# Hybrid RG-LRU and pooling layer: bias sums formed from the other side and at other places, opening matmuls reordered, last output blocks finished another way

## The chip, the core and the metric

The kernel runs on one core of one Trainium2 chip. The metric is device time in microseconds (us) of one execution of the whole kernel, as the median of several runs.

## What is computed

One layer with 1024 frames, a model width of 1024 and float32 data. The reference, cut to its core:

```python
h = x @ w_in + b_in                       # 1024 x 6144: xa | za | xb | zb | ga | gb
xa = causal_conv4(xa)
ya = RG_LRU(xa) * silu(za)                # gates, then a scan along the frames
yb = multiscale_pool(xb) * silu(zb)       # windows 2, 4, 8, 16
merged = sigmoid(ga) * (ya @ w_proj_a) + sigmoid(gb) * (yb @ w_proj_b)
y = merged @ w_out + b_out
out = layer_norm(alpha * x + y)           # alpha = 2 ** 0.25, gain and bias rows
```

So there are nine products of 1024x1024 by 1024x1024 (six of them in the first line) and some smaller ones. The last line is the place of the biased input: the kernel forms x + b_out / alpha once, in DRAM, multiplies it by alpha when the first product of `w_out` is added, and then adds the other products.

## The kernel before

**Products.** Each float32 operand is split into a high and a low part (a cast on ScalarE, ACT, and a subtraction on VectorE, DVE), and a product is three matmuls: high by high, high by low, low by high. Each 1024-cubed product is cut into 2x2 blocks and formed from seven block products instead of eight, numbered j = 1 to 7, which needs sums of blocks of both operands first. The sums of the projection weights, of ya and yb and of `w_out` are formed from DRAM to DRAM by transfers on GpSimd's queue (POOL), where a second transfer accumulates onto what the first one wrote.

**Order.** The program is recorded into a plan (`Plan`), and a planner writes it out in an order of its own for each engine; for that reason nearly all instructions carry line L394 in the profile and are told apart by the names of their tiles. Work goes through these stages: the opening (group 0, gate columns of `w_in`, while x arrives), 22 groups for the columns of branches A, G and B, each with products, an elementwise front and stores, the merge (`steps`: seven block products for a, then seven for b), the output product (`O_STEPS`, in the order 1, 6, 7, 5, 3, 4, 2) and the layer norm of the last row blocks.

**The queue of jobs.** The DRAM sums stand in a list, `jobs`. `run_jobs(n, i, t)` (L663) is called once in each group i: ACT copies a column of a fresh tile (`pace`), POOL copies that (`paced`), which makes POOL wait until the group has come so far, and then POOL issues the next n transfers. They run strictly in the list's order, and a transfer that reads or accumulates onto what another wrote waits for it, with all that stand behind it on POOL. In a group of kind B n is 3, else 2. What is in the list is, in order: sums of the weights for a and b (`weight_sums`, L680), sums for ya as far as its first half allows (`input_sums1`, L713) and for `w_out` (`output_sums`, L690) once half of the branch A is done, then the rest for ya (`input_sums2`, L718), the biased input (`biased_input`, L702), and the sums for yb (t1b, t3b, t2b, t4b), which are put there in branch B. The merge ends it: what is left is run at two steps.

**The biased input.** `biased_input` loads the row b_out in two halves, scales it by 1 / alpha on ACT and stores it to `bias` in DRAM. Then for each of four blocks of 256 rows one job copies x to `xb` and one accumulates the broadcast bias row onto it, all on POOL's queue, blocks 2, 3, 0, 1. It is called after the last column block of A. At the merge's end SyncE (SP) loads the eight row blocks `z` from `xb`.

**The opening.** Two weight columns, n = 0 and n = 1, each have a tile `w0h` and `w0l`. For four quarters (kh, h) of x, `split_x` splits the quarter and `mm0(q, kh, h, n)` (L997) adds three matmuls for column n. `split_w0(1, 0, 1)` splits the first part of the second weights; it stands after the first quarter's matmuls for n = 0.

**The layer norm.** `o_norm(s)` (L1433) takes the mean and variance of row block s, centres it and multiplies by the gain row. For blocks 0 to 5 (`BY_DMA`, L1409) the bias row has been written to `out` by SP beforehand, ACT multiplies by the reciprocal deviation, and POOL accumulates the block onto `out`. For blocks 6 and 7 DVE multiplies and adds the bias row, and SP stores each half. DVE centres into `zt[s]` itself, which ACT's Square also reads. Block 7's statistics come from BN_STATS and BN_AGGR on DVE instead.

Of the kernel before, what the change touches and what calls it, by code (L numbers as in the profile page):

```python
# [11 lines left out]
F32 = mybir.dt.float32  # L12
F32R = mybir.dt.float32r
AF = mybir.ActivationFunctionType
ALU = mybir.AluOpType

P = 128
S = 1024
D = 1024
# [387 lines left out]
def layer_kernel(ctx: ExitStack, tc: tile.TileContext, xq, x, w_in, par, wg, w_pool, wpa, wpb, w_out, rows, out):  # L407
# [235 lines left out]
    def both(t, m1):  # L643
        for sl in HALF:
            V.tensor_tensor(t[:, sl], t[:, sl], m1, ALU.add)
# [24 lines left out]
    def add_to(t, u):  # L670
        nc.gpsimd.dma_start(t, u, accum_op=ALU.add, max_dma_last_dim=2048)
# [27 lines left out]
    xb_d = [dram.tile([2 * P, D], F32, tag=f"xb{i}", name=f"xb{i}") for i in range(4)]  # L699
    bias_d = dram.tile([1, D], F32, tag="bias", name="bias")  # L700

    def biased_input():  # L702
        for sl in HALF:
            t = epool.tile([1, H], F32, tag="e", name=f"bias_{sl.start}")
            nc.sync.dma_start(t, rows[0:1, sl])
            A.mul(t, t, 1.0 / ALPHA)
            nc.sync.dma_start(bias_d[:, sl], t)
        for i in (2, 3, 0, 1):
            jobs.append(lambda i=i: nc.gpsimd.dma_start(xb_d[i], x[2 * P * i:2 * P * (i + 1), :]))
            jobs.append(lambda i=i: add_to(xb_d[i], bias_d.to_broadcast((2 * P, D))))  # L710


    def input_sums1(n):  # L713
# [46 lines left out]
    def a_gates(c, xc, xh, xl, sz):  # L760
        gh, gl = gw[c]
        if c + 1 < NK:
            load_g(c + 1)

        r, i = kt(f"r{c}"), kt(f"i{c}")
        for h in range(2):
            pg = [bank(f"ps_g{c}_{h}_{n}") for n in range(2)]
            for k, (w, m) in enumerate(((gh, xh), (gh, xl), (gl, xh))):
                for n in range(2):
                    nc.tensor.matmul(pg[n], w[HEAD[n], :], m[HEAD[n], HALF[h]], start=k == 0, stop=k == 2)  # L770
            for t, half, ps, s, cb in ((r, LO, pg[0], LO, C_BR), (r, HI, pg[1], HI, C_BR),
                                       (i, LO, pg[0], HI, C_BI), (i, HI, pg[1], LO, C_BI)):
                A.activation(t[half, HALF[h]], ps[s], AF.Sigmoid, bias=par_sb[s, cb + c:cb + c + 1])

        a = kt(f"a{c}")
        A.activation(a, r, AF.Exp, scale=sc_a[:, c:c + 1])
        t = r
        A.activation(t, r, AF.Tanh, scale=sc_t[:, c:c + 1])
        V.tensor_tensor(i, i, xc, ALU.mult)
        V.scalar_tensor_tensor(i, a, 1.0, i, ALU.add, ALU.mult)  # L780
        V.scalar_tensor_tensor(a, a, 1.0, t, ALU.add, ALU.mult)
        V.tensor_scalar(a, a, -1.0, 1.0, ALU.mult, ALU.add)
        A.activation(t, t, AF.Sqrt)
        V.tensor_tensor(i, i, t, ALU.mult)
        hs = t
        V.tensor_tensor_scan(hs, a, i, 0.0, ALU.mult, ALU.add)
        V.tensor_tensor(hs, hs, sz, ALU.mult)
        A.mul(hs[:, negative(c)], hs[:, negative(c)], -1.0)
        store_y("a", c, hs)
        if c == KQ - 1:  # L790
            input_sums1("a")
            output_sums()
        elif c == NK - 1:
            input_sums2("a")
            biased_input()


    sg_d = {sec: dram.tile([NK, P, S], F32, tag=f"sg{sec}", name=f"sg{sec}") for sec in (GA, GB)}
# [198 lines left out]
    def mm0(q, kh, h, n):  # L997
        sl = slice(q * P, (q + 1) * P)
        passes(ps0[n][h], (wh[n][:, kh, sl], wl[n][:, kh, sl]), quarter(q, kh, h),
               q == 0 and kh == h, q == KQ - 1 and kh != h)  # L1000
# [78 lines left out]
    for kh, h in ((0, 0), (1, 1), (0, 1), (1, 0)):  # L1079
        split_x(0, kh, h)  # L1080
        mm0(0, kh, h, 0)
        if kh == h == 0:
            split_w0(1, 0, 1)
        mm0(0, kh, h, 1)
    split_w0(0, 1, KQ)
    parts(1, lambda: split_w0(1, 1, KQ))
    w = weights_steps(1)
# [60 lines left out]
    due, pools, last, ends, W = {}, {}, [], [], {}  # L1148
    weight_sums("a", wpa)
    weight_sums("b", wpb)  # L1150
    for i in range(1, len(order)):
        kind, c = order[i]
        if i == 1:
            W[2] = load_group(2, w_next, ("4", "75", "63"))
        elif i + 1 < len(order):
            W[i + 1] = load_group(i + 1)
        if kind == "B" and c % 2 == 1:
            load_wp(c // 2)
        if i == 1:
            tiles = tiles0  # L1160
        elif kind == "A":
            tiles, takes = a_outputs(c)
        elif kind == "B":
            tiles, takes = b_outputs(c)
        else:
            finish, takes = g_outputs(GA if c < 4 else GB, c % 4)
        if i > 1:
            g = Group(f"{kind}{c}", W.pop(i), X, *takes)

        def heads(at=pools):  # L1170
            for f in at.pop(i, []):
                f()

        def between():
            heads(due)
            if prev_m3:
                prev_m3()
            if prev_end and i > 2:
                prev_end()

        if i == 1:
            prev_m3 = None
        elif i >= len(order) - 2:
            g.sums(between, heads)
            prev_m3 = None
            last.append(g)
        else:
            g.m1()
            g.m2()
            if i == 2:  # L1190
                rest = first_rest()
                next(rest)
            g.m7()
            between()
            g.m6()
            if i == 2:
                next(rest)
                prev_end()
            g.m4()
            heads()  # L1200
            g.m5()
            prev_m3 = g.m3
        if i >= 2:
            run_jobs(3 if kind == "B" else 2, i, g.t7)
        if kind == "A":
            def prev_end(c=c, tiles=tiles, i=i):
                front = a_front(c, *tiles)
                due.setdefault(i + 2, []).append(lambda: a_gates(c, *front, tiles[1]))
        elif kind == "B":
            def prev_end(c=c, tiles=tiles, i=i):  # L1210
                for _ in b_front(c, *tiles):
                    pass
                if c % 2 == 1:
                    pools.setdefault(i + 2, []).append(lambda: b_pool(c // 2))
        else:
            prev_end = finish
        if i >= len(order) - 2:
            ends.append((c, *tiles))
            prev_end = None
# [186 lines left out]
    nc.sync.dma_start(g_row, rows[1:2, :].to_broadcast((P, D)))  # L1406
    nc.sync.dma_start(be_row, rows[2:3, :].to_broadcast((P, D)))

    BY_DMA = (0, 1, 2, 3, 4, 5)  # L1409
    for s in BY_DMA:  # L1410
        nc.sync.dma_start(out[s * P:(s + 1) * P, :], rows[2:3, :].to_broadcast((P, D)))
    acc = const.tile([P, 2 * NK], F32, name="o_acc")
# [20 lines left out]
    def o_norm(s):  # L1433
# [7 lines left out]
        else:  # L1441
# [3 lines left out]
            A.activation(sq, zt[s], AF.Square, bias=nm, accum_out=var)  # L1445
            A.activation(sd, var, AF.Sqrt, bias=eps, scale=1.0 / D)
            mean, op = nm, ALU.add
        for sl in sls:
            V.scalar_tensor_tensor(zt[s][:, sl], zt[s][:, sl], mean, g_row[:, sl], op, ALU.mult)
        V.reciprocal(sd, sd)  # L1450
        if s in BY_DMA:
            A.mul(zt[s], zt[s], sd)
            add_to(out[s * P:(s + 1) * P, :], zt[s])
            return
        for sl in sls:
            V.scalar_tensor_tensor(zt[s][:, sl], zt[s][:, sl], sd, be_row[:, sl], ALU.mult, ALU.add)
            nc.sync.dma_start(out[s * P:(s + 1) * P, sl], zt[s][:, sl])

    def o_product(ps, j, g, start, stop, sl=slice(0, H)):
        for q in range(KQ):  # L1460
# [106 lines left out]
```

## Time and profile before

| what | value |
|---|---|
| median of three runs | 750.65 us (748.11, 750.65, 752.86) |
| the profiled execution's own time | 748.43 us |
| its span in the trace | 746.6 us, so 1.83 us lie around it |
| TensorE (PE) busy | 733.2 us (98%) |
| weight load (PEld), DVE, ACT, POOL busy | 599.9 (80%), 600.0 (80%), 457.4 (61%), 76.0 (10%) us |
| DMA | 158.46 MB, mean 212 GB/s |

The span runs from the first to the last instruction. PE is busy all the time but for a start, an end and a few gaps, so what matters is where PE waits, where its clock is not granted in full, and how long the work takes that follows the last matmul. The other engines run beside it and have pauses.

### The profile page before, as it was taken

The page shows a single profiled execution, that of the slowest core. Times are in us where ns is not written, and L with a number is a line of the kernel's source. Part 1 is how long each engine was busy: PE and PEld are TensorE (multiplying, and loading weights), DVE is VectorE, ACT ScalarE, POOL GpSimd, SP SyncE. Part 2 cuts the span into 40 slices and gives each one's busy share as a digit, 9 for nine tenths or more (in the row PEclk, how much of TensorE's full clock was granted, in tenths as well). Part 3 has the DMA queues.
Part 4 walks back from the last instruction along what each step waited for, and adds up shares of the span by engine and source line. Part 5 has one row for each costly group of instructions (what it writes and reads, how often), then busy time and mean ns, then how long its engine had stood idle before and what let it go on. Part 6 is the DMA issues. An engine that isn't in the chain of part 4 may idle for free.

```text
span 746.6 us, 8782 instructions
## 1 busy us (share of the span) xinstructions
PE 733.2 (98%) x3248; PEld 599.9 (80%) x3248; DVE 600.0 (80%) x746; ACT 457.4 (61%) x585; POOL 76.0 (10%) x125
## 2 busy tenths in 40 slices
PE   8999999999999999999999999999999999999995
PEld 6888888888787888788888888887888888888884
DVE  7999696969596968787977768856978886999766
ACT  7676959686868777788744445526563546324472
POOL 0171011111101011010012111110001000000021
PEclk9999999999999999999999999999999999999998
DMA  9337868676836957667187978999699998759365
GB/s 336 116 117 175 225 171 227 140 241 167 237 97 169 346 152 207 180 183 191 51 196 156 246 190 231 226 321 396 216 323 331 305 270 292 269 203 244 119 108 118
DMA packets 62435, 158.46 MB, mean 212 GB/s; under 512 B 4276, under 2 KB 7476, under 8 KB 62264
## 3 DMA queue, kind: packets, MB, share of 16 engines
q1 hardware_dynamic: 41880, 102.06, 38.9%
q0 software_dynamic: 19968, 55.58, 34.7%
q8 instruction: 25, 0.41, 0.2%
q10 hardware_dynamic: 544, 0.26, 0.1%
q14 instruction: 18, 0.15, 0.1%
HBM read 136.91 MB, written 76.55 MB: 286 GB/s over the span
## 4 chain that ended last, share of the span: by engine, by line
PE 95%; DMA 3%; DVE 1%; ACT 0%; DVEq 0%; ACTq 0%; issue 0%
PE a_A L394 11%; PE a_G L394 10%; PE a_B L394 10%; PE oa L394 6%; PE pa_b L394 6%; PE c_B L394 6%; PE c_A L394 6%; PE pa_a L394 5%; PE c_G L394 5%; PE ps_pool L394 3%; PE pc_b L394 3%; PE pc_a L394 3%; PE e_A L394 3%; PE ps_s L394 3%; PE oc L394 3%; PE e_G L394 3%
## 5 line engine op out<-in xcount | busy, mean ns | idle before, releaser
L394 ACT ACT_TABLE_LOAD x38 | 48.8, 1283 | 2.7 <-issue 2.0
L394 DVE TENSOR_TENSOR i<-i,xc 128x1024 f32<-128x1024 f32 x8 | 9.8, 1225 | 28.3 <-ACT i L394 28.3
L394 DVE SCALAR_TENSOR_TENSOR xc<-xp,par_sb,xc 128x1024 f32<-128x1024 f32 x24 | 30.7, 1279 | 0.3
L394 POOL COPY paced<-pace 128x1 f32<-128x1 f32 x21 | 12.1, 574 | 174.1 <-ACT pace L394 174.1
L394 PE MATMUL pa_a<-oh,oh 128*128 128x512 f32 x64 | 25.7, 402 | 1.3 <-ACT oh L394 1.3
L394 PE MATMUL pa_a<-oh,ol 128*128 128x512 f32 x64 | 25.6, 400 | 0.5 <-DVE ol L394 0.5
L394 PE MATMUL pa_a<-ol,oh 128*128 128x512 f32 x64 | 25.5, 398 | 0.0
L394 PE MATMUL pa_b<-oh,oh 128*128 128x512 f32 x64 | 24.9, 389 | 0.0
L394 PE MATMUL pa_b<-ol,oh 128*128 128x512 f32 x64 | 24.9, 389 | 0.0
L394 PE MATMUL pa_b<-oh,ol 128*128 128x512 f32 x64 | 24.9, 389 | 0.0
L394 ACT ACTIVATE r<-ps_g,par_sb 64x512 f32<-64x512 f32 x32 | 21.9, 684 | 2.1 <-PE ps_g L394 1.2
L394 ACT ACTIVATE i<-ps_g,par_sb 64x512 f32<-64x512 f32 x32 | 21.9, 684 | 1.9 <-DVE r L394 1.4
L394 ACT ACTIVATE zb<-zb,par_sb 128x1024 f32<-128x1024 f32 (+1 forms) x16 | 15.0, 938 | 13.0 <-DVE zb L394 12.9
L394 PE MATMUL c_A<-x64h,wd_A 128*128 128x512 f32 x64 | 21.0, 389 | 0.0
L394 PE MATMUL c_B<-x64h,wd_B 128*128 128x512 f32 x64 | 21.0, 389 | 0.0
L394 PE MATMUL ps_pool<-mixh,wp 128*128 128x512 f32 x64 | 20.6, 394 | 0.0
L394 POOL DMA_DIRECT2D out<-z x6 | 7.1, 1190 | 124.7 <-ACT z L394 124.7
L394 PE MATMUL e_B<-x,wah_B 128*128 128x512 f32 x64 | 19.7, 389 | 0.0
L394 PE MATMUL e_A<-x,wah_A 128*128 128x512 f32 x64 | 19.7, 389 | 0.0
L394 PE MATMUL c_G<-x64h,wd_G 128*128 128x512 f32 x56 | 18.4, 389 | 0.0
L394 DVE TENSOR_TENSOR_SCAN r<-a,i 128x1024 f32<-128x1024 f32 x8 | 18.3, 2283 | 0.1
L394 PE MATMUL e_G<-x,wah_G 128*128 128x512 f32 x56 | 17.2, 389 | 0.0
(522 smaller groups left out, 2544.6 us busy)
## 6 DMA issues: line engine op xcount, KB each, us to landing
sg<-sg SPq DMA_DIRECT2D x16, 512.0 KB, 4.9
ra_A<-in_w_in SPq DMA_DIRECT2D x8, 512.0 KB, 9.5
rb_A<-in_w_in SPq DMA_DIRECT2D x8, 512.0 KB, 6.6
ya<-r SPq DMA_DIRECT2D x8, 512.0 KB, 5.0
ra_B<-in_w_in SPq DMA_DIRECT2D x8, 512.0 KB, 6.0
rb_B<-in_w_in SPq DMA_DIRECT2D x8, 512.0 KB, 5.3
yb<-zb SPq DMA_DIRECT2D x8, 512.0 KB, 6.5
xb<-bias POOLq DMA_DIRECT2D x4, 1024.0 KB, 12.6
```

Source lines behind the costliest of these rows:

```text
L394: getattr(getattr(nc, t.op[0]), t.op[1])(*a, **k)
```

## The change

Five edits, in the words of the code:

1. `biased_input` takes the blocks as an argument. The bias row is prepared at its first call only. For each block one job now does both steps: SP writes the broadcast bias row to `xb`, then POOL accumulates x onto it. It is called for blocks 2 and 3 right after the weight sums, and for 0 and 1 after `output_sums` in the fourth column block of A.
2. `run_jobs` takes 2 jobs in each of the groups below 10 and 3 from there on, whatever the kind.
3. In the opening the second weights are split, and their matmuls for the first quarter added, after the second quarter's matmuls for n = 0.
4. Block 6 joins `BY_DMA`: its bias row is written to `out` by SP, and its end is one multiplication on ACT and one accumulating transfer on POOL.
5. `o_norm` centres into a tile of its own, `y`, save for the last block.

```diff
--- before.py
+++ after.py
@@ -699,15 +699,18 @@
     xb_d = [dram.tile([2 * P, D], F32, tag=f"xb{i}", name=f"xb{i}") for i in range(4)]
     bias_d = dram.tile([1, D], F32, tag="bias", name="bias")
 
-    def biased_input():
-        for sl in HALF:
+    def biased_input(blocks):
+        for sl in HALF if not src.get("bias") else ():
+            src["bias"] = True
             t = epool.tile([1, H], F32, tag="e", name=f"bias_{sl.start}")
             nc.sync.dma_start(t, rows[0:1, sl])
             A.mul(t, t, 1.0 / ALPHA)
             nc.sync.dma_start(bias_d[:, sl], t)
-        for i in (2, 3, 0, 1):
-            jobs.append(lambda i=i: nc.gpsimd.dma_start(xb_d[i], x[2 * P * i:2 * P * (i + 1), :]))
-            jobs.append(lambda i=i: add_to(xb_d[i], bias_d.to_broadcast((2 * P, D))))
+        for i in blocks:
+            def both(i=i):
+                nc.sync.dma_start(xb_d[i], bias_d.to_broadcast((2 * P, D)))
+                add_to(xb_d[i], x[2 * P * i:2 * P * (i + 1), :])
+            jobs.append(both)
 
 
     def input_sums1(n):
@@ -790,9 +793,9 @@
         if c == KQ - 1:
             input_sums1("a")
             output_sums()
+            biased_input((0, 1))
         elif c == NK - 1:
             input_sums2("a")
-            biased_input()
 
 
     sg_d = {sec: dram.tile([NK, P, S], F32, tag=f"sg{sec}", name=f"sg{sec}") for sec in (GA, GB)}
@@ -1079,9 +1082,11 @@
     for kh, h in ((0, 0), (1, 1), (0, 1), (1, 0)):
         split_x(0, kh, h)
         mm0(0, kh, h, 0)
-        if kh == h == 0:
+        if kh == h == 1:
             split_w0(1, 0, 1)
-        mm0(0, kh, h, 1)
+            mm0(0, 0, 0, 1)
+        if kh or h:
+            mm0(0, kh, h, 1)
     split_w0(0, 1, KQ)
     parts(1, lambda: split_w0(1, 1, KQ))
     w = weights_steps(1)
@@ -1148,6 +1153,7 @@
     due, pools, last, ends, W = {}, {}, [], [], {}
     weight_sums("a", wpa)
     weight_sums("b", wpb)
+    biased_input((2, 3))
     for i in range(1, len(order)):
         kind, c = order[i]
         if i == 1:
@@ -1201,7 +1207,7 @@
             g.m5()
             prev_m3 = g.m3
         if i >= 2:
-            run_jobs(3 if kind == "B" else 2, i, g.t7)
+            run_jobs(2 if i < 10 else 3, i, g.t7)
         if kind == "A":
             def prev_end(c=c, tiles=tiles, i=i):
                 front = a_front(c, *tiles)
@@ -1406,7 +1412,7 @@
     nc.sync.dma_start(g_row, rows[1:2, :].to_broadcast((P, D)))
     nc.sync.dma_start(be_row, rows[2:3, :].to_broadcast((P, D)))
 
-    BY_DMA = (0, 1, 2, 3, 4, 5)
+    BY_DMA = (0, 1, 2, 3, 4, 5, 6)
     for s in BY_DMA:
         nc.sync.dma_start(out[s * P:(s + 1) * P, :], rows[2:3, :].to_broadcast((P, D)))
     acc = const.tile([P, 2 * NK], F32, name="o_acc")
@@ -1445,16 +1451,17 @@
             A.activation(sq, zt[s], AF.Square, bias=nm, accum_out=var)
             A.activation(sd, var, AF.Sqrt, bias=eps, scale=1.0 / D)
             mean, op = nm, ALU.add
+        y = zt[s] if s == last else xt(f"y{s}", F32, (P, S))
         for sl in sls:
-            V.scalar_tensor_tensor(zt[s][:, sl], zt[s][:, sl], mean, g_row[:, sl], op, ALU.mult)
+            V.scalar_tensor_tensor(y[:, sl], zt[s][:, sl], mean, g_row[:, sl], op, ALU.mult)
         V.reciprocal(sd, sd)
         if s in BY_DMA:
-            A.mul(zt[s], zt[s], sd)
-            add_to(out[s * P:(s + 1) * P, :], zt[s])
+            A.mul(y, y, sd)
+            add_to(out[s * P:(s + 1) * P, :], y)
             return
         for sl in sls:
-            V.scalar_tensor_tensor(zt[s][:, sl], zt[s][:, sl], sd, be_row[:, sl], ALU.mult, ALU.add)
-            nc.sync.dma_start(out[s * P:(s + 1) * P, sl], zt[s][:, sl])
+            V.scalar_tensor_tensor(y[:, sl], y[:, sl], sd, be_row[:, sl], ALU.mult, ALU.add)
+            nc.sync.dma_start(out[s * P:(s + 1) * P, sl], y[:, sl])
 
     def o_product(ps, j, g, start, stop, sl=slice(0, H)):
         for q in range(KQ):
```

How the planner writes this out is shown at three places. The first is TensorE in the opening; `ps_s0_0` is the bank for weight column 0 and half 0, and x13h, x13l, w0h, w0l are the high and low parts. Before:

```order
L394 MATMUL ps_s0_0_148<-x13h0_141,w0h0_143 128x512
L394 MATMUL ps_s0_0_148<-x13l0_145,w0h0_143 128x512
L394 MATMUL ps_s0_0_148<-x13h0_141,w0l0_150 128x512
L394 MATMUL ps_s1_0_161<-x13h0_141,w0h1_153 128x512
L394 MATMUL ps_s1_0_161<-x13l0_145,w0h1_153 128x512
L394 MATMUL ps_s1_0_161<-x13h0_141,w0l1_164 128x512
L394 MATMUL ps_s0_1_169<-x13h0_141,w0h0_143 128x512
L394 MATMUL ps_s0_1_169<-x13l0_145,w0h0_143 128x512
L394 MATMUL ps_s0_1_169<-x13h0_141,w0l0_150 128x512
```

After:

```order
L394 MATMUL ps_s0_0_148<-x13h0_141,w0h0_143 128x512
L394 MATMUL ps_s0_0_148<-x13l0_145,w0h0_143 128x512
L394 MATMUL ps_s0_0_148<-x13h0_141,w0l0_150 128x512
L394 MATMUL ps_s0_1_161<-x13h0_141,w0h0_143 128x512
L394 MATMUL ps_s0_1_161<-x13l0_145,w0h0_143 128x512
L394 MATMUL ps_s0_1_161<-x13h0_141,w0l0_150 128x512
L394 MATMUL ps_s1_0_169<-x13h0_141,w0h1_153 128x512
L394 MATMUL ps_s1_0_169<-x13l0_145,w0h1_153 128x512
L394 MATMUL ps_s1_0_169<-x13h0_141,w0l1_163 128x512
```

The two matmul groups of column 0 now stand together, and those of `ps_s1_0`, which need the second weights, come third.

The second place is POOL's queue, from the last copy that paces the biased input to the first sum for yb. Before:

```order
L394 COPY paced_613<-pace_610 128x1
L394 DMA xb2_3351<-bias_2805 256x2x512
L394 DMA xb3_3508<-in_x 16x16384
L394 DMA xb3_3508<-bias_2805 256x2x512
L394 COPY paced_613<-pace_610 128x1
L394 DMA xb0_3655<-in_x 16x16384
L394 DMA xb0_3655<-bias_2805 256x2x512
L394 DMA xb1_3810<-in_x 16x16384
L394 COPY paced_613<-pace_610 128x1
L394 DMA xb1_3810<-bias_2805 256x2x512
L394 COPY paced_613<-pace_610 128x1
```

After, the same queue just ahead of the first sum for yb:

```order
L394 COPY paced_616<-pace_612 128x1
L394 DMA xb0_2799<-in_x 512x512
L394 DMA xb1_2801<-in_x 512x512
L394 COPY paced_616<-pace_612 128x1
L394 DMA t2a_2378<-ya_1016 512x512
L394 DMA t3a_2284<-ya_1016 512x512
L394 DMA t4a_2390<-ya_1016 512x512
L394 COPY paced_616<-pace_612 128x1
L394 DMA t4a_2390<-ya_1016 512x512
L394 COPY paced_616<-pace_612 128x1
L394 DMA t1b_3740<-yb_3443 512x512 x2
L394 DMA t3b_3839<-yb_3443 512x512
```

Block by block, the copy of x and the bias behind it, with four pacing copies, stood ahead of t1b. Now the blocks 0 and 1 are one accumulation each and stand ahead of the second sums for ya, and only those stand ahead of t1b.

The third place is DVE at the end of the program, from the centring of block 6 to the statistics of block 7 (oc, oe are banks of the last two products, row1 and row2 the gain and bias rows). Before:

```order
L394 SCALAR_TENSOR_TENSOR z6_5273<-z6_5273,nm6_5905,row1_5455 128x512 x2
L394 TENSOR_TENSOR z7_5279<-z7_5279,oc_3_5594 128x512
L394 RECIPROCAL sd6_5916<-sd6_5916 128x1
L394 SCALAR_TENSOR_TENSOR z6_5273<-z6_5273,sd6_5916,row2_5457 128x512
L394 TENSOR_TENSOR z7_5279<-z7_5279,oe_3_0_5921 128x256
L394 SCALAR_TENSOR_TENSOR z6_5273<-z6_5273,sd6_5916,row2_5457 128x512
L394 BN_STATS stats_5954<-z7_5279 128x6
L394 TENSOR_TENSOR z7_5279<-z7_5279,oe_3_256_5937 128x256
L394 BN_STATS stats_5954<-z7_5279 128x6 x3
L394 BN_AGGR mv7_5961<-stats_5954 128x2
```

After:

```order
L394 SCALAR_TENSOR_TENSOR y6_5909<-z6_5267,nm6_5906,row1_5449 128x512 x2
L394 RECIPROCAL sd6_5920<-sd6_5920 128x1
L394 TENSOR_TENSOR z7_5273<-z7_5273,oc_3_5589 128x512
L394 BN_STATS stats_5935<-z7_5273 128x6 x2
L394 TENSOR_TENSOR z7_5273<-z7_5273,oe_3_0_5925 128x256
L394 BN_STATS stats_5935<-z7_5273 128x6
L394 TENSOR_TENSOR z7_5273<-z7_5273,oe_3_256_5944 128x256
L394 BN_STATS stats_5935<-z7_5273 128x6
L394 BN_AGGR mv7_5961<-stats_5935 128x2
```

The two passes over z6 with the bias row are gone, and two of the four BN_STATS of block 7 now come before the sum with the bank oe.

## Rows read from the trace of the kernel before

**Rows 1.** Waits of TensorE: engine, tile, releaser: us in total, times, longest.
```profile
PE pa_a L394 <- ACT oh L394: 1.3, 1, 1.3
```
**Rows 2.** Chain that ended last, in order of time: start us, us, what.
```profile
490.02 14.01 DMA wa1r<-in_wpa
...
513.27 10.88 PE pe_a L394 x48
```
**Rows 3.** TensorE's timeline at the merge's first step: start us, us, instruction, idle before.
```profile
503.43 0.39 PE L394 MATMUL pa_a<-oh,ol 128*128 128x512 f32 x1
...
506.42 0.63 PE L394 MATMUL pa_a<-oh,ol 128*128 128x512 f32 x1 [0.53 <-DVE ol L394]
...
510.16 0.39 PE L394 MATMUL pa_a<-oh,ol 128*128 128x512 f32 x1
```
**Rows 4.** Windows: stretch, length, busy PE, PEld, DVE, ACT, POOL, PEclk, DMA, GB/s.
```profile
505.00:510.00 5.00, 4.32 (x11) 3.13 (x12) 3.58 (x3) 3.04 (x4) 0.00 (x0) 0.66 1.34 545
```
**Rows 5.** POOL's timeline: the first sum for yb.
```profile
469.53 2.35 POOL L394 DMA_DIRECT2D t1b<-yb  x1
...
487.38 1.03 POOL L394 DMA_DIRECT2D t1b<-yb  x1 [15.51 <-DMA t1b<-yb]
```
**Rows 6.** DMA queues: packets, MB, share of the 16 engines' span.
```profile
q1 hardware_dynamic: 41880, 102.06, 38.9%
q0 software_dynamic: 19968, 55.58, 34.7%
```
**Rows 7.** Timelines of ACT and of SP's queue before and at the merge's start.
```profile
437.33 0.19 ACT L394 COPY pace<-m_B 128x1 f32<-128x1 f32 x1
...
448.02 4.12 SPq L394 DMA_DIRECT2D yb<-zb  x2
...
464.24 0.36 SPq L394 DMA_DIRECT2D xa1r<-ya  x1
```
**Rows 8.** DMA issues: count, KB each, median us from issue to landing.
```profile
yb<-zb SPq DMA_DIRECT2D x8, 512.0 KB, 6.5
xb<-bias POOLq DMA_DIRECT2D x4, 1024.0 KB, 12.6
...
out<-in_rows SPq DMA_DIRECT2D x6, 512.0 KB, 11.4
...
out<-z POOLq DMA_DIRECT2D x6, 512.0 KB, 5.9
```
**Rows 9.** Timelines of TensorE and DVE in the opening.
```profile
7.45 0.50 PE L394 MATMUL ps_s<-x13h,w0h 128*128 128x512 f32 x1 [1.64 <-ACT w0h L394]
...
13.54 0.50 PE L394 MATMUL ps_s<-x13h,w0l 128*128 128x512 f32 x1
...
11.67 1.82 DVE L394 TENSOR_TENSOR w0l<-w0r,w0h 128x768 fp32r<-128x768 f32 x2
```
**Rows 10.** Timelines of TensorE and DVE at the end of the program.
```profile
734.83 1.42 DVE L394 SCALAR_TENSOR_TENSOR z<-z,nm,row 128x512 f32<-128x512 f32 x2 [1.37 <-ACT sq L394]
...
737.82 0.28 PE L394 MATMUL oe<-wo2h,o2l 128*128 128x256 f32 x1
...
738.95 0.40 DVE L394 TENSOR_TENSOR z<-z,oe 128x256 f32<-128x256 f32 x1
739.27 1.07 DVE L394 BATCH_NORM_STATS2 stats<-z 128x6 f32<-128x256 f32 x3
740.38 0.26 DVE L394 BATCH_NORM_AGGREGATE mv<-stats 128x2 f32<-128x24 f32 x1
```
**Rows 11.** The weight block rb_A6: its load on SP, cast, low part, first use.
```profile
228.00 0.33 SPq L394 DMA_DIRECT2D rb_A<-in_w_in  x1
...
251.65 0.60 ACT L394 CAST wd_A<-rb_A 128x512 fp32r<-128x512 f32 x1
...
259.67 1.22 DVE L394 TENSOR_TENSOR wbl_A<-rb_A,wbh_A 128x1024 fp32r<-128x1024 f32 x1
...
269.66 0.39 PE L394 MATMUL c_A<-x57h,wbl_A 128*128 128x512 f32 x1
```

## The prediction

> **What bounds the kernel now.** I began with the page: TensorE is busy for 98% of the span, so a gain must come from its waits, from its clock, or from what lies behind its last matmul. The next view was the list of TensorE's waits. Only four are named, and all others together are nothing: two in the opening (1.64 us of them for the second weights, [rows 9]) and two at the merge's first step, of which the first stands in [rows 1] and the second, 0.53 us, in [rows 3]. In the chain of waits the merge's step is the one place far from start and end where a transfer stands: the second half of `wa1r`, issued at 490.02, takes 14.01 us to land [rows 2].
>
> What that costs is more than the waits. A matmul of this kind starts every 10.88/48 = 0.2267 us [rows 2]. The last one in step began at 503.43, so the next was due at 503.66; with the one at 510.16 twelve have begun since (11 of them in 505 to 510, [rows 4]). Without the stall the twelfth, eleven pitches behind the first, would have begun at 503.66 + 11 x 0.2267 = 506.15 instead of 510.16: the loss is 4.0 us. 1.3 + 0.53 = 1.8 us of it are the named waits; in most of the rest the matmuls start slowly, and the granted clock in 505 to 510 is 0.66 as a mean, between the two levels of 1.2 and 2.4 GHz [rows 4]. TensorE had just stood still for the first time in the middle of the program. So one late landing is paid for twice.
>
> Why does it land late? In POOL's timeline the first sum for yb, `t1b`, starts at 469.53 only, and its second part at 487.38 [rows 5]. The pacing copy for it was ready at 437.33 [rows 7]; the biased input stood ahead of it. So t1b and t3b, of 1 MB each, are in flight when wa1r is.
>
> **The end.** TensorE's last matmul ends at 737.82 + 0.28 = 738.10, but DVE adds the last bank at 738.95 only, and aggregates at 740.38 [rows 10]. DVE is the bound there, busy with block 6.
>
> **The change part by part.**
>
> *Biased input and jobs.* The bytes are the same, but they leave the stretch ahead of t1b: three pacing copies and eight transfers of 1 MB fall away there. What is t1b then late for? It reads yb, of which the last two blocks are issued from 448.02 on, over 4.12 us, and take 6.5 us [rows 7, 8]: the last, issued at about 451.8, is there at 458.3. That is 469.53 - 458.3 = 11.2 us earlier. To see if wa1r is then in time I add up what the 16 engines have to move. The queue of POOL holds them for 34.7% of 746.6 us; with 55.58 MB, that is 53 transfers of 1 MB (2^20 bytes), 4.89 us of all 16 engines for each; SP's queue, 38.9% and 102.06 MB, comes to 1.49 us for 512 KB [rows 6]. Test on before: from 490.02 two transfers of 1 MB (t1b's second, t3b) and three of 512 KB (wa1r and two that come behind it) give 9.78 + 4.47 = 14.3 us; measured were 14.01 [rows 2]. After: from 458.3 to 490.02 the engines have 31.7 us. POOL's five (t1b twice, t3b, t2b, t4b) and nine of SP between the one at 464.24 [rows 7] and wa1r's second half, both ends of the list counted but that half, take 5 x 4.89 + 9 x 1.49 = 37.9 us. So 6.2 us are left at 490.02, and wa1r lands by 490.02 + 6.2 + 1.5 = 497.7 if all that goes first. TensorE needs it by 503.66, less the cast; a tile half as large takes ACT 0.60 us [rows 11], so about 1.2: 502.4. The slack is over 4 us: the stall goes, -4.0 us. Bounds: 0, if the transfers still collide (a rival below), and -4.0, since no more is lost there.
>
> What hides the rest: blocks 2 and 3 are now summed in group 10, where SP issues two broadcasts of 1 MB ahead of the load of rb_A6 at 228.00 [rows 11], and blocks 0 and 1 in group 15, with the same pattern. The load is first read by ACT at 251.65, 23.65 us later. The broadcast of a row has two rows to bound it: six of 512 KB from SP, issued in a run, land 11.4 us after issue in the median, [rows 8]; if the fourth of them marks that, each takes 3 us, and 1 MB takes 6 us; on POOL, accumulating, 1 MB took 12.6 us [rows 8]. By the first, rb_A6 is delayed by about 12 us and is in time. I take that one, as it is the same kind of transfer on the same queue: 0 us. The three pacing copies that fall away were on engines that wait for nothing there: 0 us.
>
> *Opening.* The wait of 1.64 us for the second weights gets three matmuls that used to stand behind it, 3 x 0.2267 = 0.68 us. But the gap is only passed on: the matmul at 13.54 reads `w0l`, and DVE produces its second part over 1.82 us from 11.67, so until 13.49 [rows 9]. Its order and ACT's are not touched. TensorE comes to that matmul 0.68 us earlier, and waits. So 0; bounds -0.68 (if the low parts are ready earlier than the row says) and +0.1 (a late start of one matmul).
>
> *The end.* For block 6 two DVE passes are left out, and DVE's order is such that half of the statistics of block 7 are done before the last bank. Then the last add starts as the matmul ends, 738.14; it takes 739.27 - 738.95 = 0.32 to the next instruction, one BN_STATS of 1.07/3 = 0.36 follows, and the aggregation starts at 738.82 instead of 740.38 [rows 10]: -1.56, of which I take -1.5 for the start of one instruction more. The chain behind it (two passes, a store) is as it was. What is next in line is block 6 itself. Even if its centring ends as late as in before, at 734.83 + 1.42 = 736.25, and ACT takes as long for its multiplication as DVE for that, POOL issues at 737.7, and the accumulation lands 5.9 us later [rows 8], at 743.6. Block 7's store, in before the last thing, ends behind that, at 746.6 - 1.5 = 745.1. Bounds: -1.5, and +3.7 if the accumulation takes the 12.6 us of [rows 8] and lands at 750.3; the six transfers of `out<-z` are of exactly this kind, so I give that little room. A separate y lets DVE centre without waiting for ACT's Square (1.37 us of idle time in [rows 10]), but before block 7 nothing waits for that: 0.
>
> *Bias row for block 6.* One broadcast more of 512 KB, 3 us by the estimate above, behind six others on SP, ahead of the loads of the last weights; these have over 10 us: 0.
>
> *Sum.* 748.43 (the profiled execution) - 4.0 - 1.5 - 0 = 742.9. The median of the runs is 2.2 us above that execution; I keep half of that, 1.1, since it was one of the faster executions but not faster than the fastest run shown: 744.0 us.
>
> **Rivals.**
>
> *A, the collision stays* (0.2). POOL's transfers come at other times, but the same bytes go through the same engines, and what now runs at group 22 may meet wa1r as t2b and t4b. For it: 6.2 us of work are left at 490.02 by my own sum, and SP's loads of the merge come then too. Against: 4 us of slack. It would leave only the end's gain: 748.43 - 1.5 = 746.9, so 748.0 in the median. The Trainium skill says of this ("DMA: Bandwidth & Descriptors", Rules for kernel authors) that spreading DMAs over several issuing engines brings no bandwidth, as all run on the same 16 engines and interleave. The trace agrees where 14.3 us of summed work gave a landing in 14.01; by the rule the move of work from POOL to SP alone would bring nothing, and what counts is the time at which it runs.
>
> *B, slower: the broadcasts hold up the weights* (0.06). SP's two writes of 1 MB stand ahead of rb_A6. TensorE needs its low part at 269.66; DVE's pass ends at 259.67 + 1.22 = 260.89, so 8.8 us later would do, and rb_A6 is in time if it lands by 251.65 + 8.8 = 260.4 [rows 11]. From that point on each us costs one. At 12.6 us for each broadcast, with the two accumulations of 4.89 us interleaved, it lands at 228.0 + 25.2 + 9.8 + 1.5 = 264.5: a wait of about 4, and as much as 1.9 us for the clock, as at the merge. The pattern comes twice (rb_A6, rb_B2): 742.9 + 2 x 5.9 = 754.7, and 755.8 in the median. For it: nothing in before writes a broadcast row of this size from SP. Against: the row of SP's six broadcasts.
>
> *C, the opening yields too* (0.12): the low parts are not what holds TensorE at 13.54, and 0.68 us more comes off: 742.2, or 743.3 in the median.
>
> **How the numbers follow.** The forecast has 0.62: 744.0 us. About 1% (7.5 us) is what a measurement of this kernel can tell from no change, and the whole gain is 5.5 us, or 0.7%. Even with C the sum is 6.2, and all waits of TensorE, its clock at the merge and DVE's late end together are hardly more than that. So the likeliest outcome is within 1%. Faster by over 1% needs C, or the runs to scatter in its favour: 0.25. Slower by over 1% needs B at both places with longer waits than worked out there: 0.05. The rest, 0.7, is within 1%. The range: down to 741.5, which is C and somewhat of scatter; up to 748.5, which holds A. B is left out above it.
>
> **What would show it.** Right: t1b starts on POOL at about 458, wa1r's second half lands within 9 us of its issue, and TensorE's waits for `oh` and `ol` at the merge are gone, with the clock at 1.0 in that stretch. The aggregation starts 0.7 us after the last matmul ends. In the opening the wait for the second weights is shorter, but a new one stands ahead of the first matmuls that read the second part of `w0l`. Wrong: a wait of TensorE for `oh` remains at the merge, or moves to the step behind it; TensorE waits for wd_A or wbl_A at group 12 or so; the chain ends with POOL's accumulation of block 6.

## The result and the profile after

The changed kernel takes 744.75 us in the median of seven runs (742.62 to 745.87), the kernel before 750.65 us (747.90 to 755.54). The ratio is 0.9933 with an interval of 0.9908 to 0.9959: faster, by 0.7%, and the forecast was 744.0. The profiled execution took 744.67 us, with a span of 742.9. Against the 746.6 of before that is 3.7 us, so the two profiled executions lie closer together than the medians.

First the waits of TensorE in the changed kernel (engine, tile, releaser: us in total, times, longest):

```profile
PE ps_warm L394 <- DVE xp L394: 1.4, 1, 1.4
PE a_B L394 <- DVE zb L394: 0.8, 1, 0.8
PE a_B L394 <- ACT u_B L394: 0.4, 1, 0.4
```

The waits for `oh` and `ol` at the merge [rows 1, 3] are gone. In their place there are two that before did not have, in a_B, which is in branch B. To see what each is worth, one follows the same piece of work through the chain of waits of both executions. Of the changed kernel's chain (start us, us, what):

```profile
28.77 2.72 PE a_A L394 x12
...
324.33 2.72 PE a_B L394 x12
...
362.93 5.73 PE a_B L394 x24
368.66 2.72 PE e_B L394 x12
...
510.53 10.88 PE pe_a L394 x48
```

and of the kernel before:

```profile
29.07 2.72 PE a_A L394 x12
...
324.71 2.72 PE a_B L394 x12
...
361.88 5.44 PE a_B L394 x24
367.32 2.72 PE e_B L394 x12
```

The piece at 324 starts 0.38 us earlier than before (most of it from the opening), e_B at 368.66 starts 1.34 later: between them 1.72 us are lost. The two named waits are 1.1 of it (0.75 and 0.37 on TensorE's timeline); the rest is in matmuls that start late by less than the list names. The granted clock is 1.00 there (350 to 370), so unlike at the merge no slower clock is paid for on top. The piece `pe_a` [rows 2] starts 513.27 - 510.53 = 2.74 earlier: from e_B on, 4.08 are won. From there to the last matmul nothing changes, and behind it the end is 0.95 shorter: 746.6 - 738.10 = 8.50 before, 742.9 - 735.35 = 7.55 after. The sum: -0.38 + 1.72 - 4.08 - 0.95 = -3.7, which is the difference of the two spans.

How the 4.08 come about is seen on POOL's timeline of the changed kernel, beside [rows 5]:

```profile
456.60 0.66 POOL L394 DMA_DIRECT2D t1b<-yb  x1 [17.50 <-issue]
463.90 1.02 POOL L394 DMA_DIRECT2D t1b<-yb  x1 [6.65 <-DMA t1b<-yb]
...
475.40 0.52 POOL L394 DMA_DIRECT2D t2b<-t1b  x1 [8.80 <-DMA t1b<-yb]
475.91 0.50 POOL L394 DMA_DIRECT2D t4b<-t1b  x1
```

where the last of these sums, in the kernel before, stood at

```profile
502.90 0.50 POOL L394 DMA_DIRECT2D t4b<-t1b  x1
```

The second half of wa1r, on the timelines of SP's queue and of ACT in the changed kernel:

```profile
491.30 0.37 SPq L394 DMA_DIRECT2D wa1r<-in_wpa  x1
...
497.87 1.06 ACT L394 CAST oh<-wa1r 128x1024 fp32r<-128x1024 f32 x1 [2.30 <-DMA wa1r<-in_wpa]
```

t1b begins 12.9 us earlier than before, and the last of the sums for yb leave POOL at 476, ahead of wa1r and not behind it. ACT's cast, which waits for the second half of wa1r, starts 6.6 us after that was issued; before, it took 14.01 us to land [rows 2]. The window of [rows 4], in the changed kernel:

```profile
505.00:510.00 5.00, 5.00 (x24) 4.14 (x23) 5.00 (x6) 4.03 (x5) 0.00 (x0) 1.00 1.05 388
```

24 matmuls in the five microseconds instead of 11 [rows 4], at a granted clock of 1.00 (2.4 GHz all through) instead of 0.66.

Now the new wait. On DVE, on the timeline of the changed kernel:

```profile
352.76 0.69 DVE L394 TENSOR_TENSOR zb<-c_B,u_B 128x512 f32<-128x512 f32 x1 [5.17 <-DMA sg<-sg]
```

and in what the tile `sg` answers there, between 330 and 360:

```profile
who waited for it (us, times):
  DVE zb L394: 5.2, 1
  ACT L394: 3.1, 1
...
DMA to landing us min/median/max: 12.9/13.3/13.8
```

`sg<-sg` is a store of two finished gate tiles, 512 KB each, to DRAM. `zb` needs nothing of it but its place: both come from one ring of ten working tiles (`kt`), and until the store has read the old tile DVE may not write the new one. The two broadcasts of the bias were issued on SP at 323.07, 16.6 us ahead of these stores, and with them the transfer engines had no pause when the stores came. The window of 340 to 350 in the changed kernel, whose last two columns are DMA share and GB/s:

```profile
340.00:350.00 10.00, 10.00 (x45) 8.26 (x45) 4.74 (x3) 8.50 (x11) 0.00 (x0) 1.00 1.03 294
```

and in the kernel before:

```profile
340.00:350.00 10.00, 10.00 (x46) 8.29 (x45) 6.78 (x6) 8.34 (x10) 0.00 (x0) 1.00 0.65 193
```

DVE stands still for 5.17 us, and TensorE, which waits for DVE to empty a bank, for a part of it.

The end, on the timelines of TensorE and DVE of the changed kernel, beside [rows 10]:

```profile
735.07 0.28 PE L394 MATMUL oe<-wo2h,o2l 128*128 128x256 f32 x1
...
735.38 0.42 DVE L394 TENSOR_TENSOR z<-z,oe 128x256 f32<-128x256 f32 x1 [0.55 <-PE oe L394]
735.84 0.43 DVE L394 BATCH_NORM_STATS2 stats<-z 128x6 f32<-128x256 f32 x1
736.30 0.26 DVE L394 BATCH_NORM_AGGREGATE mv<-stats 128x2 f32<-128x24 f32 x1
```

DVE now waits for TensorE, not the other way round, and aggregates 0.95 us after the last matmul instead of 2.28. That is 1.33 nearer, of which 0.95 arrive at the end of the span: what follows the start of the aggregation took 742.9 - 736.30 = 6.60 us instead of 746.6 - 740.38 = 6.22. Over all 14 executions with a trace that tail takes 6.2 to 6.6 us, with the old end (6.2 to 6.5) as with the new one (6.3 to 6.6), so the other 0.38 is mostly scatter.

### The profile page after: what moved, and what is told of

The parts are those of the page before. It is cut to its first block, busy times and chain, and to the rows that moved or that the text cites. A ratio compares the mean times of both kernels' runs of the same rounds, so it can differ in the third digit from the quotient of the medians.

```text
span 742.9 us, 8776 instructions
## 1 busy us (share of the span) xinstructions
PE 732.6 (99%) x3248; PEld 599.4 (81%) x3248; DVE 600.5 (81%) x744; ACT 458.7 (62%) x583; POOL 70.0 (9%) x119
## 4 chain that ended last, share of the span: by engine, by line
PE 96%; DVE 1%; DMA 1%; issue 1%; ACT 0%; SPq 0%; DVEq 0%
PE a_A L394 11%; PE a_G L394 10%; PE a_B L394 10%; PE oa L394 6%; PE pa_a L394 6%; PE pa_b L394 6%; PE c_A L394 6%; PE c_B L394 5%; PE c_G L394 5%; PE ps_pool L394 3%; PE oc L394 3%; PE pc_b L394 3%; PE pc_a L394 3%; PE e_B L394 3%; PE e_A L394 3%; PE e_G L394 3%
## 5 line engine op out<-in xcount | busy, mean ns | idle before, releaser
L394 POOL COPY paced<-pace 128x1 f32<-128x1 f32 x18 | 9.7, 541 | 124.4 <-ACT pace L394 124.4
L394 POOL DMA_DIRECT2D out<-y x7 | 8.5, 1210 | 131.2 <-ACT sd L394 115.7
L394 PE MATMUL e_G<-x,wah_G 128*128 128x512 f32 x56 | 17.2, 389 | 0.0
## 6 DMA issues: line engine op xcount, KB each, us to landing
xb<-bias SPq DMA_DIRECT2D x4, 1024.0 KB, 13.4
```

The lines of the kernel that those rows point to most:

```text
L394: getattr(getattr(nc, t.op[0]), t.op[1])(*a, **k)
```

## Experiments

Twelve runs were made in three groups, each group on one chip beside the kernel before; one of them is the changed kernel once more, and one repeats another. The kernel before had a median of 747.95, 747.91 and 747.68 us there, so ratios are compared, not times across groups.

**The parts alone.** The biased input with the counts of jobs, the kernel before otherwise:

```diff
+        for i in blocks:
+            def both(i=i):
...
+            biased_input((0, 1))
...
-            biased_input()
...
+    biased_input((2, 3))
...
-            run_jobs(3 if kind == "B" else 2, i, g.t7)
+            run_jobs(2 if i < 10 else 3, i, g.t7)
```

> Edits 1 and 2 alone (biased input and the counts of jobs), opening and end as before. Theory: t1b starts at about 457 and TensorE's waits for wa1r's parts are gone, -4.1 us; two new waits of TensorE at a_B near 354 and 363, because stores of sg land late beside the broadcasts of the bias, cost +1.7: span about 744.2 (-2.4). Rival (the new waits come from the shift of the opening and not from the broadcasts): they are absent, span about 742.5.

Measured: 745.68 us, ratio 0.9968 (0.9954 to 0.9982), span 745.0. Its waits of TensorE:

```profile
PE ps_warm L394 <- DVE xp L394: 1.4, 1, 1.4
PE a_B L394 <- DVE zb L394: 1.4, 1, 1.4
PE ps_s L394 <- ACT w0h L394: 1.4, 1, 1.4
PE a_B L394 <- ACT u_B L394: 0.4, 1, 0.4
```

t1b starts at 457.48, the merge's waits are gone, and both waits at a_B are there although the opening is the old one. So they belong to this part, and the rival falls. From the piece at 324 to e_B 2.36 us are lost, 0.64 more than in the changed kernel's trace, which is most of the 0.8 by which the span is above the expected one.

The opening alone:

```diff
-        if kh == h == 0:
+        if kh == h == 1:
             split_w0(1, 0, 1)
-        mm0(0, kh, h, 1)
+            mm0(0, 0, 0, 1)
+        if kh or h:
+            mm0(0, kh, h, 1)
```

> Edit 3 alone. Theory: the start of TensorE's steady run moves by 0.3 us only, since w0l's second part on DVE still holds it at about 13.2 to 13.5; the waits at the merge's first step stay; span 746.3, not to be told from before by the time. Rival: the three matmuls are gained in full, -0.7, with no wait ahead of the matmuls that read w0l's second part.

Measured: 746.76 us, ratio 0.9974 (0.9953 to 0.9994), span 745.0. The interval just leaves out no change, but the trace doesn't put the gain in the opening. On its timelines of DVE and TensorE:

```profile
11.72 1.82 DVE L394 TENSOR_TENSOR w0l<-w0r,w0h 128x768 fp32r<-128x768 f32 x2
...
13.59 0.50 PE L394 MATMUL ps_s<-x13h,w0l 128*128 128x512 f32 x1
...
28.96 0.39 PE L394 MATMUL a_A<-x13h,wah_A 128*128 128x512 f32 x1
```

In before these stood at 11.67, 13.54 and 28.91. The chain reaches the last e_B ahead of the merge at 487.55 (before: 487.50), and TensorE's last matmul ends 1.60 us earlier than before: what this execution won it won at the merge, where its waits were shorter. Why the median is lower, the trace of one execution can't show. Over all 14 executions with a trace the start of the first a_A is that of DVE's w0l plus 17.22 to 17.32 us, in the old order (11.67 and 28.91; 11.62 and 28.85; 10.92 and 28.15; 11.64 and 28.88; 11.51 and 28.73; 11.79 and 29.11) as in the new one (11.37 and 28.60; 11.72 and 28.96; 11.74 and 28.96; 11.60 and 28.84; 10.93 and 28.18; 10.91 and 28.15; 11.09 and 28.31; 11.16 and 28.38). When DVE comes to w0l varies by 0.9 us between executions, in either order.

The end alone:

```diff
+    BY_DMA = (0, 1, 2, 3, 4, 5, 6)
...
+        y = zt[s] if s == last else xt(f"y{s}", F32, (P, S))
```

> Edits 4 and 5 alone. Theory: the aggregation starts 0.95 us after TensorE's last matmul instead of 2.28, -1.0 to -1.3 us in all; the merge's waits stay; span about 745.5. Rival (the transfer of block 6 on POOL's queue ends last): the end moves by less than 0.5.

Measured: 747.51 us, ratio 0.9993 (0.9979 to 1.0006), span 746.5. TensorE's last matmul ends at 739.23 in its trace, and DVE has on its timeline

```profile
740.19 0.26 DVE L394 BATCH_NORM_AGGREGATE mv<-stats 128x2 f32<-128x24 f32 x1
```

so 0.96 us later. The step does what was expected of it; 746.5 - 739.23 = 7.3 us lie behind the last matmul instead of 8.5. In this execution's span it is not seen, because the merge's wait, which this kernel still has, was 2.4 us for `oh` alone. In the median a gain of 1 us can't be told from none: the interval reaches from 1.6 us faster to 0.4 slower. So the gain of the end is read from traces and not shown by a time. And of the two edits in it, the tile y alone:

```diff
+        y = zt[s] if s == last else xt(f"y{s}", F32, (P, S))
```

> The separate tile y alone, block 6 ending on DVE and SP as before. Theory: DVE's two passes with the bias row over block 6 remain between the last matmul and the statistics; the aggregation starts 2 us or more after TensorE's last matmul, time as before. Rival (the wait for ACT's Square is what made DVE late): it starts within 1.3 us of it.

Measured: 746.87 us, ratio 0.9995 (0.9971 to 1.0019). In its trace the last matmul ends at 743.19, and then

```profile
740.44 0.75 DVE L394 SCALAR_TENSOR_TENSOR y<-y,sd,row 128x512 f32<-128x512 f32 x1
...
741.71 0.74 DVE L394 SCALAR_TENSOR_TENSOR y<-y,sd,row 128x512 f32<-128x512 f32 x1
...
744.59 0.26 DVE L394 BATCH_NORM_AGGREGATE mv<-stats 128x2 f32<-128x24 f32 x1
```

Here the theory failed: the aggregation is 1.40 behind the matmul, not 2 or more. The passes with the bias row are still there, but as DVE need not wait for Square, they are over before TensorE is done. So 0.9 of the 1.3 us come with y, and 0.45 more when block 6 ends by transfer, each by one trace; the transfer without y was not run.

The counts of jobs alone:

```diff
-            run_jobs(3 if kind == "B" else 2, i, g.t7)
+            run_jobs(2 if i < 10 else 3, i, g.t7)
```

> Edit 2 alone on the kernel before: counts of jobs. Theory: the biased input is a chain of eight transfers of which each pair takes about 16 us, and starts at about 405 in any case, so t1b starts at 465 or later and wa1r lands 13 us or more after its issue; the waits at the merge's first step stay, the time is within 1 us of before. Rival (the counts alone free t1b): t1b by 460, the waits gone, 3 us less.

Measured: 747.47 us, ratio 0.9989 (0.9975 to 1.0003). t1b starts at 469.10, and TensorE waits 2.1 and 0.5 us at the merge. The theory held: by themselves the counts don't free the merge. The new places without the new counts were not run.

**What the biased input cost before.** It is left out, so the output lacks b_out:

```diff
-            biased_input()
...
-        nc.sync.dma_start(zt[s], xb_d[s // 2][(s % 2) * P:(s % 2 + 1) * P, :])
+        nc.sync.dma_start(zt[s], x[s * P:(s + 1) * P, :])
```

> The kernel before with the biased input left out: the output lacks b_out, z is loaded from x. Theory: t1b starts at about 457, no wait at the merge, none at a_B; 3 to 4.5 us less than before, the opening and the end as in before. Rival (the collision at the merge comes from t1b's own transfers): the wait stays, less than 1.5 us gained.

Measured: 744.35 us (744.14 to 744.46), ratio 0.9954 (0.9940 to 0.9969), so 2.3 to 4.5 us less on 747.68. t1b starts at 455.10, the second half of wa1r lands in 7.1 us, no wait at the merge and none at a_B. It also shows the scatter: five runs within 0.3 us, where 23 of before on that chip went from 745.54 to 753.00. The wait at the merge is most likely what scatters: in the six traces that have it, it is between 0.8 us (time of that execution 746.81) and 6.8 us (752.63).

**Place or form?** The new form at the old place, and the old form at the new places:

```diff
-            biased_input((0, 1))
...
             input_sums2("a")
+            biased_input((2, 3, 0, 1))
...
-    biased_input((2, 3))
```

> The changed kernel with the new form of the sum for all four blocks at the old place, behind the second sums for ya. Theory (eight transfers in turn on POOL are what held t1b; with the new form there are four that need not wait for one another): t1b starts by 465, wa1r's second half lands within 11 us, no wait at the merge, no wait at a_B near 354; 742.5 to 744. Rival (the place is what counts): t1b after 466, a wait of 1 us or more at the merge, 746 or more.

Measured: 748.80 us (745.27 to 753.65), ratio 1.0018 (0.9998 to 1.0039). Its POOL timeline:

```profile
462.39 1.86 POOL L394 DMA_DIRECT2D t1b<-yb  x1
476.47 1.02 POOL L394 DMA_DIRECT2D t1b<-yb  x1 [12.21 <-DMA t1b<-yb]
...
490.26 0.50 POOL L394 DMA_DIRECT2D t2b<-t1b  x1 [11.93 <-DMA t1b<-yb]
490.75 0.49 POOL L394 DMA_DIRECT2D t4b<-t1b  x1
```

and for the second half of its wa1r, issued at 489.45:

```profile
DMA to landing us min/median/max: 15.5/15.5/15.5
```

The theory's first number held (t1b by 465), its conclusion didn't. Seven microseconds for t1b, from 469.5 to 462.4, are worth nothing: its second part can only be issued 14.1 us after the first (7.3 in the changed kernel), and t2b and t4b start at 490, when wa1r is issued. Thirteen are worth 4.1. All 14 traces fall into two groups. In eight t1b starts between 454.88 and 457.48, and ACT's cast of the second half of wa1r starts 6.3 to 7.4 us after that was issued. In six t1b starts between 462.39 and 469.53, and it takes 13.0 to 19.5 us. Inside the second group an earlier t1b brings nothing. That looks like a threshold, with the sums for yb out of the way at 490 or not; no run lies between 457.5 and 462.4, so how sharp it is stays open. The new form alone doesn't get there, though it moves half of the transfers from POOL's queue to SP's. By the Trainium skill ("DMA: Bandwidth & Descriptors", Rules for kernel authors), issuing transfers from several engines brings no bandwidth. The ratio of 1.0018 is in line with that, though this run doesn't measure bandwidth.

The old form at the new places:

```diff
-                nc.sync.dma_start(xb_d[i], bias_d.to_broadcast((2 * P, D)))
-                add_to(xb_d[i], x[2 * P * i:2 * P * (i + 1), :])
+                nc.gpsimd.dma_start(xb_d[i], x[2 * P * i:2 * P * (i + 1), :])
+                add_to(xb_d[i], bias_d.to_broadcast((2 * P, D)))
```

> The changed kernel with the old form of the sum (POOL copies x, then accumulates the broadcast bias) at the new places. Theory (the broadcasts from SP, issued ahead of POOL's turn, delay the stores of sg): those land in 6 to 7 us, no waits at a_B near 354 and 363, t1b at about 457, time 1.3 to 2 us below the changed kernel. Rival (the place is what counts, in either form): the waits at a_B stay, and the time is the changed kernel's or more, as each block takes about 16 us on POOL.

Measured: 745.47 us (742.71 to 746.69), ratio 0.9955 (0.9938 to 0.9972). Its trace is of the fastest of its runs, with a span of 740.9. There t1b starts at 454.88 and no wait at a_B is left, as expected. But 1.3 to 2 us less than the changed kernel was expected, and the median is 1.75 above that of the changed kernel on the same chip (743.72, below), with intervals that overlap. What its slower executions wait for no trace shows. In this trace the place, with the new counts, frees the merge; the form is not needed for that.

**The new wait at a_B.** Blocks 0 and 1 are put later:

```diff
             output_sums()
-            biased_input((0, 1))
         elif c == NK - 1:
             input_sums2("a")
+            biased_input((0, 1))
```

> The changed kernel with blocks 0 and 1 of the biased input queued after the second sums for ya, so that their broadcasts run near 410 instead of 323. Theory: the stores of sg near 340 land in time, the waits at a_B near 354 and 363 are gone, t1b still starts at about 457: 1.7 us less than the changed kernel, about 743.0 in the median. Rival: the broadcasts hold up t1b or the weights there, a wait at the merge or at a later a_B returns, and the time is 744.7 or more.

Measured: 743.02 us (742.70 to 743.32), ratio 0.9932 (0.9916 to 0.9948), and t1b starts at 455.75. The tile sg, between 330 and 360:

```profile
DMA to landing us min/median/max: 6.5/6.5/6.5
```

DVE does not wait for the store, and the waits at a_B are gone, while t1b has only two transfers of the biased input ahead of it. Once more, with the changed kernel on the same chip:

> The changed kernel itself, for comparison on the same chip as the runs beside it. It shows the waits at a_B near 354 and 363, with the stores of sg landing after 13 to 14 us, and no wait at the merge's first step; 1 to 2 us slower than the run with the late blocks.

> The changed kernel with blocks 0 and 1 queued after the second sums for ya, beside the changed kernel on the same chip. Theory: 1.3 to 2.0 us less than the changed kernel. Rival (the difference of the first look was one of chips): within 0.5 of it.

Measured: the changed kernel 743.72 us (742.70 to 746.83), ratio 0.9942 (0.9921 to 0.9963); the late blocks 742.73 (742.51 to 743.57), ratio 0.9923 (0.9907 to 0.9939). They are 1.0 us apart, between the theory and the rival, and the intervals overlap. The trace of the changed kernel says why: the wait isn't there in each execution. In this one the two stores landed in 11.4 and 12.9 us, DVE waited

```profile
  DVE zb L394: 3.6, 1
```

and no wait of TensorE at a_B is named. What counts is the first store, whose place `zb` takes. In the three traces in which that is so it landed 11.4, 12.9 and 13.6 us after its issue (this one, the first of the changed kernel, the biased input alone), and from the piece at 324 to e_B 0.2, 1.72 and 2.36 us were lost: from about 11 us on each microsecond of delay costs one. So the late blocks take away a scatter upwards: on this chip five of their six runs are under 742.8, only one of the six of the changed kernel. Their ratio is the lowest of all, but its interval overlaps that of the changed kernel and that of the next run.

Last, more of the suspected traffic:

```diff
+                for _ in range(2 if i < 2 else 1):
+                    nc.sync.dma_start(xb_d[i], bias_d.to_broadcast((2 * P, D)))
```

> The changed kernel with the bias row written twice into blocks 0 and 1 (the same values), so twice the broadcast ahead of the stores of sg near 340. Theory (the stores of sg land late beside the broadcasts, and zb on DVE waits for their buffer): they land after 16 us or more, the waits at a_B near 354 and 363 together are 3 us or more, 2 to 5 us more than the changed kernel. Rival (the weights rb_B behind the broadcasts are what is late): TensorE or DVE waits for wbh_B, wd_B or wbl_B instead, and not behind a store of sg.

Measured: 742.83 us (742.63 to 743.02), ratio 0.9934 (0.9918 to 0.9950): not slower than the changed kernel. That was a miss. The stores of sg do land late, after 14.8 us, and DVE waits for them:

```profile
349.54 1.22 DVE L394 TENSOR_TENSOR i<-i,xc 128x1024 f32<-128x1024 f32 x1
354.27 0.75 DVE L394 SCALAR_TENSOR_TENSOR xbp<-e_B,par_sb,m_B 128x512 f32<-128x512 f32 x1 [3.51 <-DMA sg<-sg]
```

But the planner, with two more transfers to place, gave the working tiles out in another way: `zb` was written at 347.21 without a wait, and `xbp` got the place of sg, four instructions of DVE and 3.5 us later (it was due at 354.27 - 3.51 = 350.76). TensorE could bear that. So what a late store costs depends on when the tile that inherits its place is needed, and not on the length of the traffic alone. A price that grows with the traffic this run didn't show, as the heir changed with it.

## Why the prediction was right

Step by step:

- **The merge, -4.0.** Right: -4.08 in the trace. t1b was forecast for 458 and came at 456.60. The sum of transfers by the engines' share put the landing of wa1r's second half at 497.7; the cast that waits for it starts at 497.87.
- **The broadcasts, 0.** Here a step failed, in the sentence "0 us" for what hides the rest. Their size was about right: the trace has the landing of one of the four, the second of the pair issued from 226.31 on, 13.4 us after its own issue and 14.2 after the first one's; 12 were forecast for both. The forecast asked who waits for the load behind them, rb_A6, and that was right too: it landed 13.9 us after its issue (4.9 before), TensorE did not wait, and rival B did not come about. It didn't ask what other transfers of that time hold: stores, whose source tiles have heirs. The price was 1.72 us in the profiled execution, 0.2 in the second trace of the changed kernel.
- **The opening, 0.** Right, and rival C falls: the first a_A follows DVE's w0l by 17.2 to 17.3 us in either order. The 0.38 of the profiled execution lies in the scatter of w0l. The wait that was to stand ahead of the matmuls which read w0l's second part is not named in the list; the gap was spread over shorter ones.
- **The end, -1.5.** Right in its mechanism, too large: the aggregation came 1.33 us nearer to the last matmul. The last add was given 0.32 us and the last statistics 0.36, from rows in which the instruction behind didn't need the result; where each needs the one before, they took 0.46 each (735.38, 735.84, 736.30). The step that puts the separate y at 0, because "before block 7 nothing waits for that", was wrong: y alone brings 0.9 of the 1.33. Block 6's accumulation did not end last: POOL issued it at 734.09, and the accumulations onto `out` from 725 on landed within 5.8 us, so it was over by 740. The chain behind the aggregation was to stay as it was; it took 0.38 more in this execution, within its scatter, so 0.95 came off the span.
- **The sum.** 742.9 was forecast for an execution like the profiled one; it took 744.67. The 1.7 us between are the wait at a_B; the smaller end (0.5) and the luck in the opening (0.4) about cancel. The allowance of 1.1 us for the median hid most of that, and that is luck: the forecast of 744.0 was nearer to the median of 744.75 than its terms deserve. Before, the median was above the profiled execution, most likely because the wait at the merge scatters, and without that wait the allowance has no reason; after, the two agree to 0.1 us. The 1% that was taken for the least a measurement can tell was too much: the interval of the ratio is 0.25% to either side.
- **Rival A, the collision stays,** did not come in the changed kernel, but it is what the run with the old place shows.

## What to carry to other kernels

When a transfer is moved to a stretch with room, look there not only for the loads behind it but for the stores beside it: each holds its source tile, and the next tile in that place waits. A gain from starting a chain of transfers earlier may come all at once or not at all, where its end must be out of the way of one late load; work out the end, not the start. And take the time of a chain of dependent instructions from rows in which they depend on one another.

## What the runs showed that was not expected

TensorE's first product after the warm-up ran at different paces in executions of like kernels. In the changed kernel's trace the first matmuls start at 5.03, 5.45 and 5.88, 0.43 us apart, and from 6.73 on 0.23 apart; in before they were 0.22 to 0.24 apart from 4.96 on. The window from 5 to 6 has a granted clock of 1.00 in both, so what sets the slower pace stays open. It is not the order of the edit, since the run of the end alone, with the old opening, has 5.02, 5.45 and 5.87 too. It cost nothing here, as w0l on DVE sets what follows.
